# Four instead of two FFN pairs of layer 0 done plainly, seven by Strassen's algorithm, and the plain half-B blocks placed beside and behind a recurrence

## The chip, the cores and the metric

The kernel runs on one core of one Trainium2 chip. The metric is the device time of one execution in microseconds, the median of several runs. Before the change the median of three runs is 2479.92 us (2478.91 to 2481.79).

## What is computed

Two layers on a sequence of 1024 tokens of width 1024, all in float32. Layer 0 has a mixer (one input projection, gated spatial mixing, trailing means, one output projection), layer 1 is RWKV-7 time mixing, a recurrence over the tokens. After each mixer comes a SwiGLU FFN with 2816 hidden columns, and a last RMS norm ends the program.

```python
def swiglu(hn, w_gate, w_up, w_down):
    return (jax.nn.silu(hn @ w_gate) * (hn @ w_up)) @ w_down

# per layer
h = h + mixer(rms_norm(h, mix_norm[layer]))          # layer 0: gated mixing and pooling; layer 1: RWKV-7
h = h + swiglu(rms_norm(h, ffn_norm[layer]), ffn_w_gate[layer], ffn_w_up[layer], ffn_w_down[layer])
```

The recurrence of RWKV-7 in the reference is one step per token on a 64x64 state per head, 16 heads:

```python
sa = einsum('bhvk,bhk->bhv', state, a_t)
state = state * w_t + sa[..., None] * b_t + v_t[..., None] * k_t
y_t = einsum('bhvk,bhk->bhv', state, r_t)
```

## The kernel before, in words

**Products.** Each float32 operand is split into a high part (rounded to the fp32r format by ScalarE, `ACTIVATE`, L157) and the low rest (subtracted by VectorE, L158). One product is then three matmuls, high by high, low by high and high by low, `mm3` at L393 to L395 and `quarter` at L724 to L726. A weight block of 1024x128 is one 512 KB load into a tile `raw`, of which there are three, and is split into `whi` and `wlo`, three of each. The loads are issued on ScalarE's queue (L121), in the order of a list `plan`. `take(key)` hands out the next block of the list, splits the one behind it and issues the loads of up to two more.

**Halves.** The tokens are two halves, A (0 to 511) and B (512 to 1023). The FFN has 22 hidden blocks of 128 columns, or 11 pairs. With 1024 rows of contraction, a plain block costs 8 x 3 = 24 matmuls of 128x512 for each weight matrix (gate and up) and each half.

**Strassen.** A pair of blocks, both halves and both halves of the contraction are a 2x2 block product. `full_steps` does it with 7 products of 4 x 3 = 12 matmuls instead of 8 (`quarter`), after VectorE has made sums of the weights; `combine` has made the sums of the activations (`t1` to `t4`) before. The hidden blocks are written to memory (`hid_d`, L737) and read back (`hd`, L888) by the down projection.

**Stages, in the order of time.**
1. The mixer of layer 0.
2. `first_steps` over the list `FRONT`: half A of the plain pairs (`PLAIN`), and the first of the seven products of the pairs in `FIRST`, which is written to memory (`p1_d`) and read back later. Beside it `combine` runs on VectorE and ScalarE.
3. `full_steps` over `PORDER`: the pairs by Strassen, both halves.
4. The down projection of half A (`D0A`), then the first four groups of three blocks of half B (`D0B[0]`), beside which the projections of layer 1 for half A begin; then `project`, those projections.
5. `recur(0, ...)`: the recurrence of half A in 8 chunks of 64 tokens. Its matmuls are small (64x64 and the like, helper line L1456), depend on one another, and leave through VectorE, ScalarE and GpSimd. After every second chunk `post` normalises (`ysb`), and `turn_out` transposes and writes the result to `y_d` (L1681). Beside it `ffn(0, 1, ...)` does the plain blocks of half B: gate, up and down. `drive(dense, side, ratio)` writes out the two in turn, `ratio` units of recurrence for each unit of 24 dense matmuls, and gives the recurrence the higher priority.
6. `steps_b`: the rest of half B's down projection (`D0B[1]`, from `hid_d`), then the output projection of layer 1, which needs `y_d` back: four loads into `raw`, split into `ahi` and `alo` (`take_act`, called between the last matmuls of `steps_b`).
7. The same projections and recurrence for half B beside layer 1's FFN of half A, and the rest of the FFN.

**Order.** The kernel is written against pools of tiles with a scheduler that simulates the engines and picks, for each engine, the next instruction by priority among those that could go. So the order on each queue is the scheduler's. On an engine all is done in that order; an instruction that waits holds those behind it.

The lines that the change touches stand for stages 2, 3, 5 and 6:

```python
PLAIN = (0, 1)
FIRST = (2, 3)
PORDER = (4, 5, 6, 2, 7, 8, 9, 3, 10)
...
f = 2 * len(PLAIN)
D0P = [[2 * i, 2 * i + 1] for i in PLAIN]
D0B = [[a, a + 1, a + 2] for a in range(f, f + 12, 3)], [[a, a + 1] for a in range(f + 12, 22, 2)]
```

`D0P` are the groups of plain blocks of half B, `D0B` the groups of the others. With four plain blocks, `D0B[0]` is blocks 4 to 15 and `D0B[1]` is the pairs 16/17, 18/19 and 20/21. The hidden tiles of 16/17 come from a pool that is open during the recurrence; those of 18 to 21 from a pool `fy` that is opened after it, in the memory that the recurrence leaves.

Of the kernel before, what the change touches and what calls it, by code (L numbers as in the profile page):

```python
# [34 lines left out]


PAIRS = 11
PLAIN = (0, 1)
FIRST = (2, 3)
PORDER = (4, 5, 6, 2, 7, 8, 9, 3, 10)  # L40


@with_exitstack
def tile_trunk(
# [79 lines left out]
    def whl():  # L124
        return wst.tile([P, D], F32R, tag="whi", name="whi"), wst.tile([P, D], F32R, tag="wlo", name="wlo")
# [153 lines left out]
    while D0A[-1][-1] < 21:  # L279
        f = D0A[-1][-1] + 1  # L280
# [53 lines left out]
    def push_f(l, h, groups):  # L334
        return [lambda e=e: push_ffn_event(l, h, *e, lean=True) for e in ffn_events(groups)]

    push_beside(0, [lambda g=g: push_d(0, 1, [g]) for g in D0B[0]])
    push_proj(0, ("n0", n_d[0]))
    for e in push_f(0, 1, D0P):
        e()  # L340
    push_d(0, 1, D0B[1])
    o_first = push_o(0)
# [209 lines left out]
    hn = []  # L552
# [324 lines left out]
    def down_steps(h, groups, wslot, hslot, ahead=True, after=None, between=iter(()), at={}, first={}):  # L877

        held = {}
        for g in groups:  # L880
            for f in g:
                dests[h, f] = lambda f=f: wslot(f)

        def load(g):
            for f in g:
                if f not in held:
                    held[f] = hslot(f)
                    sp.dma_start(held[f].bitcast(F32), hid_d[h][:, f])  # L888

        def prime(n=1):  # L890
            for g in groups[:n]:
                load(g)

        def steps():
            for gi, g in enumerate(groups):
                load(g)
                wd = {f: take(("d", 0, h, f)) for f in g}
                if gi in at:
                    at[gi]()
                if ahead and gi + 1 < len(groups):  # L900
                    load(groups[gi + 1])
                for m in range(KT):
                    o = mmt()
                    ms = slice(m * P, (m + 1) * P)
                    for i, f in enumerate(g):
                        mm3(o, wd[f][0][:, ms], wd[f][1][:, ms], held[f][:, 0, :], held[f][:, 1, :], i == 0, i == len(g) - 1)
                    if gi == 0 and m in first:
                        dve.tensor_tensor(out=H[h][:, m, :], in0=first[m], in1=o, op=ALU.add)
                    else:
                        residual(m, h, o)  # L910
                    if after is not None and gi == len(groups) - 1:
                        after(m)
                    if gi == len(groups) - 1 and m % 2:
                        next(between, None)
                    yield len(g) / 8

        return prime, steps()
# [9 lines left out]
    def ffn(l, h, hn, fp, groups=GROUPS, last=False, nd=3, after=None, between=iter(())):  # L927
        dests["d"] = lambda: (fp.tile([P, D], F32R, tag="wdhi", bufs=nd, name="wdhi"),
                              fp.tile([P, D], F32R, tag="wdlo", bufs=nd, name="wdlo"))
        sg, hid, turned = {}, {}, []  # L930
        for kind, f in ffn_events(groups):
            if last and f in groups[-1] and len(turned) < 4 and (kind, f) != ("g", groups[-1][0]):
                turned.append(turn(h, len(turned)))
                if f == groups[-1][-1]:
                    turned += [turn(h, j) for j in range(len(turned), 4)] if kind == "u" else []
            if kind == "g":
                wg = take(("g", l, h, f))
                o = mmt()
                yield from dense_steps(o, *wg, *hn)
                sg[f] = fp.tile([P, HT], F32, tag="sg", bufs=2, name="sg")  # L940
                act.activation(sg[f], o, AF.Silu)
                next(between, None)
                yield FINE / KT
            elif kind == "u":
                wu = take(("u", l, h, f))
                o = mmt()
                yield from dense_steps(o, *wu, *hn)
                s = sg.pop(f)
                dve.tensor_tensor(out=s, in0=s, in1=o, op=ALU.mult)  # L949
                hi = fp.tile([P, HT], F32R, tag="hidhi", bufs=nd, name="hidhi")  # L950
                lo = fp.tile([P, HT], F32R, tag="hidlo", bufs=nd, name="hidlo")
                act.activation(hi, s, AF.Copy)  # L952
                dve.tensor_tensor(out=lo, in0=s, in1=hi.bitcast(F32), op=ALU.subtract)
                hid[f] = (hi, lo)
                next(between, None)
                yield FINE / KT
            else:
                wd = {}
                for ff in f:
                    wd[ff] = take(("d", l, h, ff))  # L960
                if last and f == groups[-1]:
                    yield from final_down(h, f, wd, hid, turned)
                    continue
                for m in range(KT):
                    o = mmt()
                    ms = slice(m * P, (m + 1) * P)
                    for i, ff in enumerate(f):
                        mm3(o, wd[ff][0][:, ms], wd[ff][1][:, ms], *hid[ff], i == 0, i == len(f) - 1)
                    residual(m, h, o)
                    if after is not None and f == groups[-1]:  # L970
                        after(m)
                    yield len(f) / 8
# [38 lines left out]
    def drive(dense_gen, side_gen=None, ratio=1.0):  # L1011

        due, left = 0.0, side_gen is not None

        def step():
            with tc.high_priority(offset=AHEAD):
                return next(side_gen, None)

        for weight in dense_gen:
            due += ratio * weight  # L1020
            while left and due > 0.0:
                cost = step()
                if cost is None:
                    left = False
                else:
                    due -= cost
        while left:
            left = step() is not None
# [880 lines left out]
    wp, wp_es = open_pool(name="wp0", bufs=1, side="left")  # L1909
    f, f_es = open_pool(name="ffn1", bufs=1, side="right")  # L1910
    _, hslot = slots_of(f, 0, 2)
    late = []
    spill_h = lambda m: sp.dma_start(h_d[1, 1][:, m, :], H[1][:, m, :])
    between = []
    prime_b, steps_b = down_steps(1, D0B[1], lambda f: whl(), lambda f: (hslot if f < 18 else late[0])(f), True, spill_h, (next(between[0]) for _ in range(4)))
    prime_b()
    drive(ffn(0, 1, nxt["hn"], f, D0P, nd=2), with_reload(hb_pool, 1, h_d[1, 0], recur(0, wp)), 9.3)
    wp_es.close()
    y, y_es = open_pool(name="y0", bufs=1, side="left")
    ys = open_act(("y", 0), y)  # L1920
    fy, fy_es = open_pool(name="ffn1y", bufs=1, side="left")
    late.append(slots_of(fy, 0, 4)[1])
    between.append(with_first(0))
    drive(steps_b)
    fy_es.close()
    f_es.close()
    ps_es.close()
    np_, np_es = open_pool(name="np1", bufs=1, side="right")
# [91 lines left out]
```

## Time and profile before

| what | value |
|---|---|
| median of 3 runs | 2479.92 us |
| the profiled execution: its time | 2477.8 us |
| its span, first to last instruction | 2476.1 us |
| mean granted TensorE clock | 0.981 |
| PE busy | 2371.4 us, 96% |
| DVE busy | 1496.4 us, 60% |
| ACT busy | 937.6 us, 38% |
| POOL busy | 215.5 us, 9% |
| read and written in HBM | 264.11 MB and 79.76 MB |

PE is TensorE's matmuls, PEld its weight loads, DVE is VectorE, ACT is ScalarE, POOL is GpSimd, SP is the engine that only issues DMAs. A busy time of PE is the time in which at least one matmul was under way; one 128x512 matmul is listed with about 394 ns, but the next starts some 0.227 us after it, so that the duration is not the price. "Idle before" and its releaser tell how long an engine stood still ahead of an instruction and what ended that. PEclk is the share of TensorE's full clock that was granted in that stretch.

### The profile page before, as it was taken

The page shows a single profiled execution, that of the slowest core. Times are in us where ns is not written, and L with a number is a line of the kernel's source. Part 1 is how long each engine was busy: PE and PEld are TensorE (multiplying, and loading weights), DVE is VectorE, ACT ScalarE, POOL GpSimd, SP SyncE. Part 2 cuts the span into 40 slices and gives each one's busy share as a digit, 9 for nine tenths or more (in the row PEclk, how much of TensorE's full clock was granted, in tenths as well). Part 3 has the DMA queues.
Part 4 walks back from the last instruction along what each step waited for, and adds up shares of the span by engine and source line. Part 5 has one row for each costly group of instructions (what it writes and reads, how often), then busy time and mean ns, then how long its engine had stood idle before and what let it go on. Part 6 is the DMA issues. An engine that isn't in the chain of part 4 may idle for free. (4 is left out here: it accounts for less than half of the span.)

```text
span 2476.1 us, 38179 instructions
## 1 busy us (share of the span) xinstructions
PE 2371.4 (96%) x15519; PEld 1948.0 (79%) x15519; DVE 1496.4 (60%) x2372; ACT 937.6 (38%) x1415; POOL 215.5 (9%) x246
## 2 busy tenths in 40 slices
PE   8999999999999999989869999999999999999998
PEld 7888888888787778768757778778888778888887
DVE  6446775666567947856758947855664446444444
ACT  6233453343313744423325744432331224322223
POOL 0200000000000023301100123201110000000001
PEclk9999999999999999999979999999999999999999
DMA  5124443333765455774435465693534322434231
GB/s 179 48 67 141 152 134 119 128 103 127 263 234 200 153 164 143 205 210 135 135 101 178 142 169 142 187 242 114 162 102 136 111 85 75 146 103 119 85 99 55
DMA packets 419248, 346.37 MB, mean 140 GB/s; under 512 B 94657, under 2 KB 364097, under 8 KB 418305
## 3 DMA queue, kind: packets, MB, share of 16 engines
q10 hardware_dynamic: 264000, 193.75, 25.9%
q1 hardware_dynamic: 155072, 150.18, 19.7%
q8 instruction: 122, 2.00, 0.3%
q14 instruction: 54, 0.43, 0.1%
HBM read 264.11 MB, written 79.76 MB: 139 GB/s over the span
## 5 line engine op out<-in xcount | busy, mean ns | idle before, releaser
L393 PE MATMUL mm<-ahi,whi 128*128 128x512 f32 x1312 | 516.4, 395 | 4.4 <-DVE h L487 2.4
L394 PE MATMUL mm<-alo,whi 128*128 128x512 f32 x1312 | 516.5, 394 | 1.1 <-DVE alo L158 1.1
L395 PE MATMUL mm<-ahi,wlo 128*128 128x512 f32 x1312 | 514.9, 393 | 0.5 <-DVE wlo L158 0.5
L157 ACT ACTIVATE whi<-raw 128x1024 fp32r<-128x1024 f32 (+1 forms) x276 | 274.3, 1000 | 566.1 <-PE mm L394 424.0
L158 DVE TENSOR_TENSOR wlo<-raw,whi 128x1024 fp32r<-128x1024 f32 (+1 forms) x276 | 319.2, 1160 | 195.0 <-ACT whi L157 173.2
L393 PEld LDWEIGHTS mm<-ahi,whi 128*128 128x128 f32 x1312 | 247.5, 189 | 59.5 <-ACT whi L157 4.2
L394 PEld LDWEIGHTS mm<-alo,whi 128*128 128x128 f32 x1312 | 247.3, 189 | 55.4 <-issue 2.4
L395 PEld LDWEIGHTS mm<-ahi,wlo 128*128 128x128 f32 x1312 | 247.4, 189 | 53.7 <-issue 1.4
L487 DVE TENSOR_TENSOR h<-h,mm 128x512 f32<-128x512 f32 x276 | 184.7, 684 | 169.1 <-PE mm L395 160.5
L393 PE MATMUL mm<-hidhi,wdhi 128*128 128x512 f32 x304 | 117.0, 394 | 7.1 <-ACT hidhi L952 2.9
L394 PE MATMUL mm<-hidlo,wdhi 128*128 128x512 f32 x304 | 119.0, 391 | 0.1
L395 PE MATMUL mm<-hidhi,wdlo 128*128 128x512 f32 x304 | 118.9, 391 | 0.0
L724 PE MATMUL mm<-ahi,whi 128*128 128x512 f32 x280 | 109.4, 391 | 0.0
L725 PE MATMUL mm<-alo,whi 128*128 128x512 f32 x280 | 109.0, 389 | 0.0
L726 PE MATMUL mm<-ahi,wlo 128*128 128x512 f32 x280 | 108.2, 389 | 0.0
L158 DVE TENSOR_TENSOR wdlo<-raw,wdhi 128x1024 fp32r<-128x1024 f32 x42 | 51.4, 1224 | 72.4 <-ACT wdhi L157 72.3
L157 ACT ACTIVATE wdhi<-raw 128x1024 fp32r<-128x1024 f32 x42 | 44.3, 1058 | 130.7 <-DMA raw<-in_ffn_w_down_dram 97.4
L949 DVE TENSOR_TENSOR sg<-sg,mm 128x512 f32<-128x512 f32 x48 | 32.9, 686 | 94.4 <-PE mm L395 94.3
L393 PE MATMUL mm<-hd,dhi 128*128 128x512 f32 x192 | 75.0, 392 | 4.1 <-ACT ahi L157 1.7
L394 PE MATMUL mm<-hd,dhi 128*128 128x512 f32 x192 | 75.2, 391 | 0.0
L395 PE MATMUL mm<-hd,dlo 128*128 128x512 f32 x192 | 74.1, 389 | 0.0
L393 PEld LDWEIGHTS mm<-hidhi,wdhi 128*128 128x128 f32 x304 | 57.0, 188 | 21.4 <-DVE h L487 4.4
(397 smaller groups left out, 4460.6 us busy)
## 6 DMA issues: line engine op xcount, KB each, us to landing
raw<-in_ffn_w_down_dram ACTq DMA_DIRECT2D x88, 512.0 KB
raw<-in_ffn_w_gate_dram ACTq DMA_DIRECT2D x72, 512.0 KB
raw<-in_ffn_w_up_dram ACTq DMA_DIRECT2D x72, 512.0 KB
hid_d<-hid SPq DMA_DIRECT2D x40, 512.0 KB
hd<-hid_d SPq DMA_DIRECT2D x30, 512.0 KB
raw<-in_ab_w_in_dram ACTq DMA_DIRECT2D x16, 512.0 KB
raw<-in_ab_w_out_dram ACTq DMA_DIRECT2D x16, 512.0 KB
raw<-in_rwkv_w_r_dram ACTq DMA_DIRECT2D x16, 512.0 KB
```

The source lines that it names most:

```text
L157: act.activation(hi, src, AF.Copy)
L158: (eng or dve).tensor_tensor(out=lo, in0=src, in1=hi.bitcast(F32), op=ALU.subtract)
L393: pe.matmul(o, whi, xhi, start=first, stop=False)
L394: pe.matmul(o, whi, xlo, start=False, stop=False)
L395: pe.matmul(o, wlo, xhi, start=False, stop=last)
L487: dve.tensor_tensor(out=H[h][:, m, :], in0=H[h][:, m, :], in1=o, op=ALU.add)
L724: pe.matmul(o, wh[:, k, :], x[0][:, k, :], start=st, stop=False, skip_group_check=True)
L725: pe.matmul(o, wh[:, k, :], x[1][:, k, :], start=False, stop=False, skip_group_check=True)
L726: pe.matmul(o, wl[:, k, :], x[0][:, k, :], start=False, stop=k == 3, skip_group_check=True)
L949: dve.tensor_tensor(out=s, in0=s, in1=o, op=ALU.mult)
```

## The change

Pairs 2 and 3 are plain too: blocks 0 to 7 are done plainly and pairs 4 to 10 by Strassen; no first products are written out and read back. In stage 5, three of the four groups of half B's plain blocks are beside the recurrence, with a ratio of 6.2 instead of 9.3, and the fourth is written behind it. `D0B[0]` becomes blocks 8 to 19 and `D0B[1]` the one pair 20/21, whose hidden tiles come from the pool that is open during the recurrence.

```diff
-PLAIN = (0, 1)
-FIRST = (2, 3)
-PORDER = (4, 5, 6, 2, 7, 8, 9, 3, 10)
+PLAIN = (0, 1, 2, 3)
+FIRST = ()
+PORDER = (4, 5, 6, 7, 8, 9, 10)
...
-    for e in push_f(0, 1, D0P):
+    for e in push_f(0, 1, D0P[:3]) + push_f(0, 1, D0P[3:]):
         e()
     push_d(0, 1, D0B[1])
...
-    late = []
     spill_h = lambda m: sp.dma_start(h_d[1, 1][:, m, :], H[1][:, m, :])
     between = []
-    prime_b, steps_b = down_steps(1, D0B[1], lambda f: whl(), lambda f: (hslot if f < 18 else late[0])(f), True, spill_h, (next(between[0]) for _ in range(4)))
+    prime_b, steps_b = down_steps(1, D0B[1], lambda f: whl(), hslot, True, spill_h, (next(between[0]) for _ in range(4)))
     prime_b()
-    drive(ffn(0, 1, nxt["hn"], f, D0P, nd=2), with_reload(hb_pool, 1, h_d[1, 0], recur(0, wp)), 9.3)
+    drive(ffn(0, 1, nxt["hn"], f, D0P[:3], nd=2), with_reload(hb_pool, 1, h_d[1, 0], recur(0, wp)), 6.2)
     wp_es.close()
     y, y_es = open_pool(name="y0", bufs=1, side="left")
     ys = open_act(("y", 0), y)
-    fy, fy_es = open_pool(name="ffn1y", bufs=1, side="left")
-    late.append(slots_of(fy, 0, 4)[1])
     between.append(with_first(0))
+    drive(ffn(0, 1, nxt["hn"], f, D0P[3:], nd=2))
     drive(steps_b)
-    fy_es.close()
     f_es.close()
```

How the scheduler orders it, at two places. First TensorE at the end of the recurrence of half A. Before, the last chunk's products of the state (`S`, `Q`, `uv`; `yp` is the output) and the last transposes (`ysb`) follow each other, and the next dense matmuls are those of the down projection from `hd`:

```order
L1456 MATMUL sm<-S,ar 64x64 x16
L1456 MATMUL sm<-Q,XT 64x64 x16
L1456 MATMUL yp<-S,ar 64x64 x16
L1456 MATMUL sm<-uv,bkt 64x64 x16
L1456 MATMUL yp<-uv,gt 64x64 x16
L1456 MATMUL sm<-ident,ysb 128x128 x8
L393 MATMUL mm<-hd,whi 128x512
L394 MATMUL mm<-hd,whi 128x512
L395 MATMUL mm<-hd,wlo 128x512
```

Now, the piece around the last transposes (buffer numbers kept, since the rows would read alike). Ahead of these rows stand 58 dense matmuls since the last `yp<-uv,gt`:

```order
L395 MATMUL mm_10961<-ahi_7768,wlo_10925 128x512
L393 MATMUL mm_11003<-hidhi_10918,whi_10957 128x512
L394 MATMUL mm_11003<-hidlo_10919,whi_10957 128x512
L395 MATMUL mm_11003<-hidhi_10918,wlo_10958 128x512
L393 MATMUL mm_11011<-hidhi_10918,whi_10957 128x512
L394 MATMUL mm_11011<-hidlo_10919,whi_10957 128x512
L395 MATMUL mm_11011<-hidhi_10918,wlo_10958 128x512
L1456 MATMUL sm_10820<-ident_63,ysb_10737 128x128
L393 MATMUL mm_11019<-hidhi_10918,whi_10957 128x512
```

What moved: 65 dense matmuls of the fourth plain group stand between the end of the last chunk and its first transpose, 6 more among the transposes, and after the last transpose 36 more of that group and the 48 of pair 20/21 come before the output projection. In the chunks between two `yp<-S,ar` there are now 30, 49, 36, 38, 53, 28 and 50 dense matmuls, where there were 28, 46, 41, 30, 23, 0 and 0.

Second, ScalarE where `y_d` is read back. Before (`raw_11022` and `raw_11096` hold the down weights of block 21 and the first weights of the output projection):

```order
L121 DMA raw_11105<-y_d0_82 128x1024
L157 ACTIVATE ahi_10931<-raw_11105 128x1024
L121 DMA raw_11129<-y_d0_82 128x1024
L157 ACTIVATE ahi_10931<-raw_11129 128x1024
L121 DMA raw_11133<-y_d0_82 128x1024
L157 ACTIVATE whi_11101<-raw_11022 128x1024
L157 ACTIVATE whi_11107<-raw_11096 128x1024
```

Now (`raw_10997` holds the down weights of block 21, `raw_11067` the first of the output projection):

```order
L121 DMA raw_11076<-y_d0_82 128x1024
L157 ACTIVATE ahi_10851<-raw_11076 128x1024
L157 ACTIVATE whi_11072<-raw_10997 128x1024
L157 ACTIVATE whi_11078<-raw_11067 128x1024
L121 DMA raw_11100<-y_d0_82 128x1024
L121 DMA raw_11104<-y_d0_82 128x1024
L157 ACTIVATE ahi_10851<-raw_11100 128x1024
L121 DMA raw_11126<-y_d0_82 128x1024
```

What moved: the split of block 21's down weights stands behind one load of `y_d` where it stood behind three, but there is only one group of the down projection left to cover that load, and that group needs these weights. Between the end of Strassen's products and the first matmul of the recurrence, TensorE's rows are the same in both.

## The prediction

> **What bounds the kernel now.** I read the page first: its span, and how much of it TensorE works.
>
> ```profile
> span 2476.1 us, 38179 instructions
> PE 2371.4 (96%) x15519; PEld 1948.0 (79%) x15519; DVE 1496.4 (60%) x2372; ACT 937.6 (38%) x1415; POOL 215.5 (9%) x246
> ```
>
> TensorE sets the time nearly everywhere, so a change counts by the matmuls that it adds and by the gaps between matmuls that it opens or closes. Then I took stretches of my own choice: Strassen's products (from 258.6), the recurrence of half A in three parts, its end, the down projection behind it, and for comparison the recurrence of half B.
>
> ```profile
> core 0: us, PE busy (x) PEld busy (x) DVE busy (x) ACT busy (x) POOL busy (x), PEclk, DMA share, GB/s
> 258.60:647.50 388.90, 388.41 (x1715) 320.92 (x1715) 255.91 (x383) 164.47 (x263) 1.12 (x2) 1.00 0.40 134
> 300.00:600.00 300.00, 300.00 (x1325) 248.43 (x1324) 196.12 (x296) 126.00 (x206) 0.00 (x0) 1.00 0.39 127
> 1119.40:1199.10 79.70, 78.79 (x1469) 65.47 (x1466) 55.06 (x125) 23.69 (x45) 10.17 (x11) 1.00 0.49 144
> 1199.10:1254.20 55.10, 44.96 (x1002) 40.83 (x998) 38.60 (x86) 17.14 (x38) 9.07 (x8) 0.84 0.44 124
> 1254.20:1279.50 25.30, 6.61 (x109) 5.71 (x106) 11.44 (x40) 4.44 (x11) 2.90 (x1) 0.63 0.18 54
> 1279.50:1307.30 27.80, 25.02 (x96) 19.50 (x97) 16.40 (x21) 7.74 (x9) 0.00 (x0) 0.91 0.58 200
> 1674.90:1831.80 156.90, 154.44 (x2621) 129.26 (x2618) 99.08 (x215) 48.89 (x93) 18.12 (x18) 0.99 0.43 127
> ```
>
> The third row has nothing but 128x512 matmuls: 300 us for 1324 of them, 0.2266 us each. That is my price of a dense matmul. Strassen's stretch runs at that pace throughout. The recurrence of half A does not: it is nearly full up to 1199, then falls to 82% at a clock of 0.84, and at its end to a quarter at 0.63.
>
> To see what a chunk costs I counted the dense matmuls in three stretches (one of the three in each triple, L394) and the recurrence's own (L1456). Each stretch begins and ends where a chunk's `yp<-S,ar` begins.
>
> ```profile
> 1119.40:1199.10 79.70, 19.28 (x48) 9.03 (x48) 1.00 0.49 144
> 1199.10:1254.20 55.10, 3.26 (x8) 1.50 (x8) 0.84 0.44 124
> 1674.90:1831.80 156.90, 43.50 (x108) 20.57 (x108) 0.99 0.43 127
> ...
> 1119.40:1199.10 79.70, 44.31 (x1324) 39.51 (x1321) 1.00 0.49 144
> 1199.10:1254.20 55.10, 39.83 (x979) 36.80 (x975) 0.84 0.44 124
> 1674.90:1831.80 156.90, 77.34 (x2297) 69.36 (x2294) 0.99 0.43 127
> ```
>
> With some 328 small matmuls a chunk these are 4, 3 and 7 chunks. Taking 144, 24 and 324 dense matmuls at 0.2266 off, a chunk's share of the time is (79.7-32.6)/4 = 11.8 us, (55.1-5.4)/3 = 16.6 us, and (156.9-73.4)/7 = 11.9 us. So a chunk with dense work to fill its waits costs 11.8, and one without costs 16.6, at a lower clock. The dense work of stage 5 ends three chunks too early.
>
> The end of that recurrence, in order of time:
>
> ```profile
> 1257.53 1.10 PE L1456 MATMUL yp<-uv,gt 128*64 128x64 f32 x32
> 1268.63 0.45 PE L1456 MATMUL sm<-ident,ysb 128*128 128x128 f32 x1 [10.00 <-DVE ysb L1662]
> 1270.79 1.73 PE L1456 MATMUL sm<-ident,ysb 128*128 128x128 f32 x7 [1.71 <-DVE ysb L1662]
> 1271.70 2.16 DVE L1678 SCALAR_TENSOR_TENSOR gch<-sm,vec,gch 128x128 f32<-128x128 f32 x8 [1.06 <-PE sm L1456]
> 1273.88 0.53 SPq L1681 DMA_DIRECT2D y_d<-gch  x1
> ...
> 1278.12 0.34 ACTq L121 DMA_DIRECT2D raw<-y_d  x1
> 1279.56 0.80 PE L393 MATMUL mm<-hd,whi 128*128 128x512 f32 x1 [7.05 <-DMA hd<-hid_d]
> 1280.16 0.63 PE L394 MATMUL mm<-hd,whi 128*128 128x512 f32 x1
> ...
> 1284.42 0.41 PE L395 MATMUL mm<-hd,wlo 128*128 128x512 f32 x1
> ...
> 1285.09 1.06 ACT L157 ACTIVATE ahi<-raw 128x1024 fp32r<-128x1024 f32 x1 [15.90 <-DMA raw<-y_d]
> ...
> 1287.44 0.33 ACTq L121 DMA_DIRECT2D raw<-y_d  x1
> ...
> 1291.01 1.06 ACT L157 ACTIVATE ahi<-raw 128x1024 fp32r<-128x1024 f32 x1 [4.86 <-DMA raw<-y_d]
> ...
> 1301.34 1.06 ACT L157 ACTIVATE ahi<-raw 128x1024 fp32r<-128x1024 f32 x1 [3.50 <-DMA raw<-y_d]
> ```
>
> TensorE stands for 10.0 us until the normalised output is there, for 1.7 in its transposes, and for 7.05 until `hd` of blocks 18 to 21 arrives: that load goes into memory that the recurrence had held, so it is issued only at its end. The next dozen matmuls then start 0.43 apart.
>
> **The change, part by part.** *More matmuls.* A weight matrix of a pair takes 7 x 12 matmuls by Strassen and 8 x 12 plainly. Two pairs and two matrices make 48 more: 48 x 0.2266 = +10.9 us. They come as 144 fewer in stages 2 and 3 (-32.6 us, in a stretch without gaps) and 192 more around the recurrence (+43.5).
>
> *The chunks.* In the order, all seven stretches between two chunks now have 28 to 53 dense matmuls. The seven cost 4 x 11.8 + 3 x 16.6 = 97.0 us before, and at 11.85 each 83.0: -14.0 us. The ends: 11.1, in which the recurrence's own matmuls alone were busy (44.31/4), gives -19; 16.6 for all gives +19. I take the middle of the two filled rows, since the same instructions ran there.
>
> *The end.* From 1254.2 to 1307.3 are 53.1 us. Their work is 96 dense matmuls, 21.8 us, and the rest of the last chunk, which costs little when the clock is full:
>
> ```profile
> 1204.19 1.15 PE L1456 MATMUL sm<-uv,bkt 128*64 128x64 f32 x32
> 1206.20 1.09 PE L1456 MATMUL sm<-ident,bk 128*128 128x128 f32 x8
> 1221.01 1.04 PE L1456 MATMUL yp<-S,ar 64*64 64x64 f32 x30
> ```
>
> With two groups of 32 at the pace of that `yp` (1.1 each), one of `uv,bkt` and eight transposes that is 4.4 us. So 53.1-21.8-4.4 = 26.9 us are lost. Now 65 dense matmuls (14.7 us) stand ahead of the first transpose, which covers the 10.0 us; `hd` of pair 20/21 is loaded before the recurrence; so no load waits for the recurrence's memory any more. I take -26.9, and what comes back of it in the next part.
>
> *What is late next.* The loads of `y_d` stand on ScalarE's queue, and behind the first of them the split of block 21's down weights, which the matmuls need. From the last transpose, at 1272.5 in the rows above: `y_d` is issued 1.4 later, its first load 5.6 later, that load lands after 3.6 (1287.44 to 1291.01), its split takes 1.1 and the weights' 1.0 (half of the first row below): 11.3 us. VectorE has a weight split ahead of `gch` (second row, 1.2):
>
> ```profile
> 1294.76 2.01 ACT L157 ACTIVATE whi<-raw 128x1024 fp32r<-128x1024 f32 x2 [2.69 <-PE mm L394]
> ...
> L158 DVE TENSOR_TENSOR wlo<-raw,whi 128x1024 fp32r<-128x1024 f32 (+1 forms) x276 | 319.2, 1160 | 195.0 <-ACT whi L157 173.2
> ```
>
> That makes 12.5. TensorE has 36 + 6 dense matmuls until then, 9.5 us. So a new wait of +3.0 us. Its ends: nothing, if the dense work runs late itself; or 6.4, if the first load takes the 7.0 it took at 1278.12, and 2.4 more for 12 matmuls at 0.43. I take 3.0, since the four `hd` loads that shared that moment are gone.
>
> [...] The row: after 7.05 us of waiting the matmuls ran at half pace until 1284.4. [...]
>
> *At nothing.* Spills and reloads of first products and of four hidden blocks go; their cover is a TensorE that is full there (388.41 of 388.90). `combine` lies beside 384 dense matmuls instead of 288, and the stretch where it fills VectorE (next rows, first) already costs TensorE nothing; were that cover gone, 24.88 of 25 us of VectorE would show. The down projection has nine groups in half B as before. The wait at the start of the recurrence (second row) stays, as the orders of TensorE and SP there are the same.
>
> ```profile
> 275.00:300.00 25.00, 25.00 (x112) 20.68 (x111) 24.88 (x38) 12.73 (x19) 0.00 (x0) 1.00 0.57 189
> ...
> 1104.14 1.06 PE L1456 MATMUL sm<-XT,gt 32*32 32x32 f32 x32 [7.29 <-ACT bkt L1514]
> ```
>
> *Sum:* +10.9 -14.0 -26.9 +3.0 = -27.0 us. The profiled execution took 2477.8 us (span 2476.1), the median is 2479.92, 2.1 above it; taken off the median: 2453.
>
> **Rivals.** *Slower: a filled chunk costs as much as an empty one.* More dense work puts more splits and residual adds on VectorE and ScalarE, and a chunk's steps queue behind them. If all seven cost 16.6, the sum is 10.9 + 7 x 16.6 - 97.0 - 26.9 + 3.0 = +6.2: 2486. It decides from 15.7 us a chunk. For it: VectorE is busy 69% in the filled stretch, and one chunk of half B, with 42 dense matmuls (the second row counts L394), came to 17.2:
>
> ```profile
> 1713.80:1740.50 26.70, 24.34 (x385) 19.66 (x381) 13.83 (x24) 7.73 (x11) 2.54 (x3) 0.94 0.60 180
> ...
> 1713.80:1740.50 26.70, 5.96 (x14) 2.92 (x14) 0.94 0.60 180
> ```
>
> Against it: the mean of the filled ones is 11.8 and 11.9 in two stretches, with that one in. 0.04.
>
> *Faster, but the output projection waits for `y_d`.* Before, the last piece was split 25.5 us after the first load's issue (1278.12 to 1301.34, and 2.3 for its two halves). Issued at 6.8 after the last transpose, that is 32.3. TensorE by then has 84 dense matmuls, the wait of 3.0 and 18 matmuls of the output projection that need only earlier pieces: 26.1. So 6.2 us more, and 2.4 at half pace: -18.4, or 2462. For it: 96 matmuls covered these loads before, now 48 and 36. Against it: two of the loads now stand next to each other in the order. [...] 0.22.
>
> *The start's wait goes too.* If the reload of `h` comes earlier relative to the first adds, 7.3 us and some half-pace matmuls go: 2444. The orders speak against it. 0.05.
>
> *No change to speak of.* Stages 2 and 3 do not shorten by 32.6 us because VectorE's sums of weights become the bound: it would need 24 us of new gaps in a stretch where VectorE is busy 256 of 389 us. 0.04; the time then is about 2478.
>
> **How the numbers follow.** The forecast, 2453, has 0.65; its own range is 2447 to 2459, from the wait at nothing and the chunks 0.4 us cheaper, to the wait at 6.4 with half pace. What this kernel's measurement can tell from no change is about 0.2%, 5 us. Forecast, `y_d` and start are faster: 0.92; no change 0.04; slower 0.04. The range takes in the start's wait on one side and `y_d` with 2 us beyond it on the other: 2443 to 2464.
>
> **What would show it.** Strassen's stretch should last some 33 us less at 0.227 a matmul. The recurrence of half A should take about 16 us longer from its first to its last small matmul, with PE near full in every 25 us and a clock of 1.00 past its start. The waits on `ysb` (11.7 us in two before) and the 7.05 on `hd` should be gone, and one of about 3 us on `whi` or `wlo` ahead of the down projection of 20/21 should be new. I am wrong if a filled chunk's share is over 13 us, if waits of over 5 us stand between the last transpose and the output projection, or if Strassen's stretch has gaps.

## The result and the profile after

The changed kernel takes 2465.49 us (median of 4 runs, 2461.21 to 2468.91) where the kernel before took 2479.41 on the same chip: a ratio of 0.9941, 95% interval 0.9926 to 0.9956, or 13.9 us less. The forecast was 27 us less, 2453, in a range of 2443 to 2464. The sign was right, the time lies 1.5 us outside the range, and half of the forecast gain is missing. The profiled execution is the fastest of the four (2461.21 us). In two runs further on, one of the kernel before and one of the regrouped kernel, the execution took nearly twice as long (4742.88 and 4764.77 us); all medians leave these out.

The page of the changed kernel, its span and its TensorE line:

```profile
span 2459.5 us, 38177 instructions
PE 2369.8 (96%) x15567; PEld 1942.6 (79%) x15567; DVE 1474.8 (60%) x2328; ACT 934.0 (38%) x1403; POOL 216.8 (9%) x246
```

There are 48 more matmuls in 1.6 us less busy time; the mean granted clock is 0.990 where it was 0.981. The stretches of it that answer to those of the prediction: Strassen's products, the seven chunk intervals of half A's recurrence, its end in two parts (up to the last small matmul, then to the first matmul of the output projection), and the third chunk interval of half B's recurrence.

```profile
core 0: us, PE busy (x) PEld busy (x) DVE busy (x) ACT busy (x) POOL busy (x), PEclk, DMA share, GB/s
258.60:615.40 356.80, 356.11 (x1574) 294.27 (x1573) 221.01 (x323) 148.66 (x235) 1.13 (x2) 1.00 0.39 128
1086.80:1235.40 148.60, 143.75 (x2580) 120.56 (x2577) 100.04 (x218) 47.36 (x90) 18.11 (x18) 1.00 0.49 141
1235.40:1261.00 25.60, 25.37 (x201) 20.39 (x196) 16.48 (x42) 10.59 (x19) 2.90 (x1) 1.00 0.19 63
1261.00:1284.20 23.20, 20.25 (x85) 15.31 (x86) 17.11 (x28) 7.69 (x9) 0.00 (x0) 1.00 0.52 169
1693.70:1725.30 31.60, 24.00 (x387) 19.97 (x385) 14.52 (x25) 9.32 (x13) 2.51 (x3) 0.84 0.55 165
```

And the dense matmuls L394 alone (one of three) in the seven intervals and in the third of half B:

```profile
1086.80:1235.40 148.60, 37.88 (x95) 17.85 (x95) 1.00 0.49 141
1693.70:1725.30 31.60, 7.02 (x15) 3.39 (x15) 0.84 0.55 165
```

The first four rows are as wanted. Strassen's stretch is 32 us shorter and still full; the seven chunks run at a clock of 1.00; behind them TensorE is busy 25.37 of 25.60 us, where before it stood for 10 us. The last row is what the prediction did not look for: in a stage whose code is unchanged, a chunk takes 31.60 us at a clock of 0.84; in the kernel before it took 26.70 at 0.94, with 43 dense matmuls in the order of either.

From the timelines come the places of a few events, in us from the start of the span. The second trace of the changed kernel is that of the first experiment.

| event | before | after | after, second trace |
|---|---|---|---|
| end of Strassen's products | 647.4 | 615.1 | 615.6 |
| first small matmul of half A's recurrence | 1088.8 | 1057.0 | 1058.3 |
| first matmul of the output projection | 1307.4 | 1284.2 | 1288.4 |
| first small matmul of half B's recurrence | 1641.1 | 1619.2 | 1625.1 |
| end of the span | 2476.1 | 2459.5 | 2468.2 |

Up to the output projection the changed kernel is 23.2 and 19.0 us ahead. From there to half B's recurrence it loses 1.3 and 3.0, and from the start of that recurrence to the end (835.0 us before) 5.3 and 8.1.

What VectorE did in that third chunk, before and then after, by the timeline:

```profile
1718.38 1.22 DVE L158 TENSOR_TENSOR wdlo<-raw,wdhi 128x1024 fp32r<-128x1024 f32 x1 [2.27 <-ACT wdhi L157]
1719.64 1.29 DVE L1503 TENSOR_TENSOR gt<-sm,gm 128x512 f32<-128x512 f32 x2
1720.85 0.68 DVE L1595 TENSOR_TENSOR Q<-S,sm 128x512 f32<-128x512 f32 x1
1724.99 1.22 DVE L158 TENSOR_TENSOR wdlo<-raw,wdhi 128x1024 fp32r<-128x1024 f32 x1 [3.47 <-ACT wdhi L157]
```

```profile
1697.26 1.23 DVE L158 TENSOR_TENSOR wdlo<-raw,wdhi 128x1024 fp32r<-128x1024 f32 x1 [1.87 <-ACT wdhi L157]
1698.52 1.29 DVE L1503 TENSOR_TENSOR gt<-sm,gm 128x512 f32<-128x512 f32 x2
1704.84 1.23 DVE L158 TENSOR_TENSOR wdlo<-raw,wdhi 128x1024 fp32r<-128x1024 f32 x1 [5.03 <-ACT wdhi L157]
1705.98 0.68 DVE L1595 TENSOR_TENSOR Q<-S,sm 128x512 f32<-128x512 f32 x1
```

The same instructions, two of them exchanged. `Q` of L1595 is the first half of the state's update (L1596 is the second). Before, it went right behind `gt`. After, a down weight's split (`wdlo`) stands ahead of it; that waits 5.03 us for ScalarE's half of the split, which waits for a load, as ScalarE's row shows. TensorE then stands for 6.20 us, and the next dense matmuls start 0.43 us apart:

```profile
1703.75 1.06 ACT L157 ACTIVATE wdhi<-raw 128x1024 fp32r<-128x1024 f32 x1 [6.52 <-DMA raw<-in_ffn_w_down_dram]
...
1706.71 1.12 PE L1456 MATMUL sm<-ident,ysb 128*128 128x128 f32 x4 [6.20 <-DVE Q L1595]
...
1708.48 0.63 PE L393 MATMUL mm<-ahi,whi 128*128 128x512 f32 x1
1708.91 0.63 PE L394 MATMUL mm<-alo,whi 128*128 128x512 f32 x1
```

`Q` started at 1705.98, as the split that stood ahead of it came to its end (1704.84 and 1.23), and VectorE did nothing else in the 5.03 us for which that split waited.

So the theory is: the change does nearly what was forecast where it was made, and the scheduler, which orders the whole program anew, put one late split ahead of the state's update in half B's recurrence. Its rival: the loss is no matter of this order, and the change is simply worth 14 us.

### The profile page after: what moved, and what is told of

Its sections match the earlier page's. It is cut to its first block, busy times and chain, and to the rows that moved or that the text cites. A ratio compares the mean times of both kernels' runs of the same rounds, so it can differ in the third digit from the quotient of the medians.

```text
span 2459.5 us, 38177 instructions
## 1 busy us (share of the span) xinstructions
PE 2369.8 (96%) x15567; PEld 1942.6 (79%) x15567; DVE 1474.8 (60%) x2328; ACT 934.0 (38%) x1403; POOL 216.8 (9%) x246
## 4 chain that ended last, share of the span: by engine, by line
PE 77%; DVE 9%; DMA 7%; ACT 3%; issue 2%; POOL 1%; ACTq 1%; SPq 0%; POOLq 0%; DVEq 0%
PE mm L393 16%; PE mm L394 16%; PE mm L395 16%; PE mm L724 5%; PE mm L726 5%; PE mm L725 5%; PE sm L1456 5%; DVE wlo L158 1%; DMA raw<-in_ffn_w_down_dram 1%; DMA raw<-y_d 1%; PE yp L1456 1%; DVE h L487 1%; DVE mix L1163 1%; ACT whi L157 1%; PE aux L1377 1%
## 5 line engine op out<-in xcount | busy, mean ns | idle before, releaser
L393 PE MATMUL mm<-ahi,whi 128*128 128x512 f32 x1376 | 541.5, 394 | 5.3 <-DVE h L487 2.8
L394 PE MATMUL mm<-alo,whi 128*128 128x512 f32 x1376 | 542.2, 394 | 1.1 <-DVE alo L158 1.1
L395 PE MATMUL mm<-ahi,wlo 128*128 128x512 f32 x1376 | 540.6, 393 | 1.1 <-DVE wlo L158 1.1
L157 ACT ACTIVATE whi<-raw 128x1024 fp32r<-128x1024 f32 (+1 forms) x280 | 281.8, 1013 | 597.1 <-PE mm L394 448.6
L158 DVE TENSOR_TENSOR wlo<-raw,whi 128x1024 fp32r<-128x1024 f32 (+1 forms) x280 | 328.9, 1179 | 216.2 <-ACT whi L157 201.1
L393 PEld LDWEIGHTS mm<-ahi,whi 128*128 128x128 f32 x1376 | 259.2, 188 | 62.9 <-ACT whi L157 5.7
L395 PEld LDWEIGHTS mm<-ahi,wlo 128*128 128x128 f32 x1376 | 259.4, 189 | 57.7 <-issue 2.2
L394 PEld LDWEIGHTS mm<-alo,whi 128*128 128x128 f32 x1376 | 259.4, 189 | 57.5 <-issue 2.4
L487 DVE TENSOR_TENSOR h<-h,mm 128x512 f32<-128x512 f32 x276 | 185.1, 684 | 164.9 <-PE mm L395 156.7
L394 PE MATMUL mm<-hidlo,wdhi 128*128 128x512 f32 x304 | 119.0, 392 | 0.1
L724 PE MATMUL mm<-ahi,whi 128*128 128x512 f32 x296 | 115.6, 390 | 0.0
L725 PE MATMUL mm<-alo,whi 128*128 128x512 f32 x296 | 115.2, 389 | 0.0
L726 PE MATMUL mm<-ahi,wlo 128*128 128x512 f32 x296 | 113.6, 389 | 0.0
L394 PE MATMUL mm<-hd,dhi 128*128 128x512 f32 x192 | 75.1, 391 | 0.0
```

The lines of the kernel that those rows point to most:

```text
L157: act.activation(hi, src, AF.Copy)
L158: (eng or dve).tensor_tensor(out=lo, in0=src, in1=hi.bitcast(F32), op=ALU.subtract)
L393: pe.matmul(o, whi, xhi, start=first, stop=False)
L394: pe.matmul(o, whi, xlo, start=False, stop=False)
L395: pe.matmul(o, wlo, xhi, start=False, stop=last)
L487: dve.tensor_tensor(out=H[h][:, m, :], in0=H[h][:, m, :], in1=o, op=ALU.add)
```

## The experiments

Times are medians; each ratio is to the kernel before on the same chip (2481 to 2483 us there). The kernels ran in three sets on two chips, so 1 or 2 us between kernels of different sets tell nothing. Where a kernel's edit adds lines, its line numbers are up to three or four higher than those of the kernel before.

**The changed kernel again.**

> The changed kernel unedited, for a second trace and more times. Theory 1: about 8 us of the forecast's 27 are lost in half B's recurrence, whose code is unchanged, because the split of a down weight now stands ahead of the third chunk's state add on VectorE. It expects about 222 us from first to last of that recurrence's small matmuls (216 before), one chunk near 31.5 us (26.8 before), and a wait of TensorE of about 6 us ahead of that chunk's transposes. Theory 2: the loss is spread over run-to-run differences of transfers and falls elsewhere in another execution; then this recurrence is back near 216 us in some execution and the time is still about 2465. Median 2465 by both.

2467.25 us (2466.40 to 2470.11), 0.9942 [0.993, 0.9954]. Theory 1 holds in the second trace: 33.6 us for the third chunk, and 7.92 us of waiting ahead of its transposes, again for `Q` behind a split. That recurrence lasted 223.7 us (222.1 in the first trace, 215.8 in the kernel before). The wait differs between the two executions, and the chunk with it.

**Another grouping, with and without the change.** In layer 1's groups beside half B's recurrence:

```diff
-[rest[i : i + 3] for i in range(0, len(rest), 3)]
+[rest[:1]] + [rest[i : i + 3] for i in range(1, len(rest), 3)]
```

> The changed kernel, with layer 1's blocks beside half B's recurrence grouped as one and then threes instead of threes from the start. In the order the state add of the third chunk then stands ahead of the weight split on VectorE, as in the kernel before. Theory 1 (the order costs 6 to 8 us): half B's recurrence 216 us or less, median 2457 to 2460. Theory 2 (the loss is elsewhere): no gain over the changed kernel beyond 2 us, 2463 to 2467.

> The kernel before with the same regrouping, so that half B's recurrence stands in the same order as in a_first. Theory 1: about the same as before, 2477 to 2482, so that a_first is 20 to 23 us faster than b_first. Theory 2: a_first is 13 to 16 us faster than b_first, as the changed kernel is than the kernel before.

2499.83 us with the change (2497.50 to 2512.34) and 2527.93 without. Both expectations for the times failed: the grouping itself costs 33 us with the change and 46 without, at the end of half B's recurrence. The difference of the two, 28.1 us, is above what either theory expects, and it settles nothing, since that end ran differently in the two traces (windows from the last `yp<-S,ar` but one to the last, with the change and without):

```profile
1791.90:1860.00 68.10, 65.50 (x425) 41.94 (x423) 19.51 (x29) 12.93 (x18) 0.00 (x0) 0.72 0.25 71
```

```profile
1820.30:1872.80 52.50, 50.42 (x427) 34.60 (x423) 19.31 (x29) 12.93 (x18) 0.00 (x0) 1.00 0.31 92
```

The clock was 0.72 in one and 1.00 in the other; more on that in the last section. What the pair does show is the third chunk itself: with the change and this grouping, `Q` stood right behind `gt` in it, and it took 23.7 us at a clock of 1.00 instead of 31.60 at 0.84.

**One subtraction moved to GpSimd, with and without the change.** The low part of one down weight (layer 1, half A, block 3); in the order no weight split stands right ahead of the third chunk's `Q` any more:

```diff
-        splits.get(key[0], lambda i, *t: split(*t))(key[1], view(raw), view(hi), view(lo))
+        if key[0] == "d" and key[1:3] == (1, 0) and key[3] in (3,):
+            split(view(raw), view(hi), view(lo), pool)
+        else:
+            splits.get(key[0], lambda i, *t: split(*t))(key[1], view(raw), view(hi), view(lo))
```

> The changed kernel with the low part of one down weight (layer 1, half A, block 3) subtracted by GpSimd instead of VectorE; in the order no weight split then stands right ahead of the third chunk's state add. Theory 1: the 31.5 us chunk is 26 us or less, the recurrence 214 to 218 us, median 2457 to 2460. Theory 2: within 2 us of the changed kernel. A third way: GpSimd's subtraction is so slow that the matmuls of block 3 wait for it, and the time is over 2467.

> The kernel before with the same GpSimd subtraction as a_pool3, so that both have half B's recurrence in nearly one order. Theory 1 (the change itself gives 20 us or more up to that recurrence, and a reordering there gave 8 back): a_pool3 is 20 to 26 us faster than this one, and this one is at most 4 us faster than before, 2476 to 2482. Theory 2 (the GpSimd subtraction helps any version by 9 us, and the change gives only 14): this one is near 2473, and a_pool3 14 to 16 us faster than it.

With the change 2457.96 us (2455.46 to 2460.15), 0.9899 [0.9885, 0.9913]; without it 2482.35, 0.9996 [0.9985, 1.0007]. The same edit gains 9.3 us in the changed kernel and nothing in the kernel before, and between the two the change is worth 24.4 us. Theory 1 holds and its rival, by which the change is worth 14 us in any order, falls. The third chunk with the change, by windows, then VectorE's rows in it:

```profile
1694.40:1716.30 21.90, 21.90 (x386) 18.53 (x384) 14.86 (x23) 8.45 (x13) 2.51 (x3) 1.00 0.71 213
```

```profile
1696.42 1.29 DVE L1506 TENSOR_TENSOR gt<-sm,gm 128x512 f32<-128x512 f32 x2 [0.51 <-PE sm L1459]
1697.63 0.68 DVE L1598 TENSOR_TENSOR Q<-S,sm 128x512 f32<-128x512 f32 x1
```

21.90 us, all of it busy, at full clock. From the start of that recurrence to the end of the span are 834.4 us, as before (835.0). The subtraction on GpSimd lay elsewhere (at 1628.4, 2.4 us long); what helped is that the splits around the third chunk were ordered anew. The limit of this proof is that the edit moved more rows of that stage than the two; the second chunk, too, went from 22.5 to 19.4 us. In the kernel before it shortened the third chunk as well, from 26.7 to 23.7 us, and that came back within the same stage: from the recurrence's start to the end it was 837.7 us there, against 835.0.

**The kernel before with all its hidden blocks read back early.** Blocks 16 to 21 into the pool that is open during half A's recurrence:

```diff
-    _, hslot = slots_of(f, 0, 2)
+    _, hslot = slots_of(f, 0, 6)
...
-    ... lambda f: (hslot if f < 18 else late[0])(f), True, ...
+    ... hslot, True, ...
-    fy, fy_es = open_pool(name="ffn1y", bufs=1, side="left")
-    late.append(slots_of(fy, 0, 4)[1])
...
-    fy_es.close()
```

> The kernel before (two plain pairs, nothing else changed) with the hidden blocks 16 to 21 read back into the pool that is open during half A's recurrence. In the order the down projection of half B (264 dense matmuls) then moves into that recurrence, 41, 37, 37, 23, 48, 33 and 45 in its seven chunks, and none are left behind its last transposes. No matmul is added. From the prediction's own rows: the chunks cost 83 instead of 97 us; behind the last chunk the waits of 10.0 and 1.7 us stay, and the output projection waits for the output's way through memory, 13 to 25 us, in place of the 7.05. In the third chunk of half B's recurrence the weight split now stands ahead of the state add, as in the changed kernel: theory 1 expects that chunk at 30 us or more and 5 to 8 us lost there, together 2472 to 2482; if that order costs nothing, the chunk is 27 us and the time 2465 to 2474.

2485.05 us, 1.0015 [1.0003, 1.0026]: slower by a little, 3 us above the expected range. It is the reverse test, since here the bad order came into a kernel without the change. The third chunk (windows), its wait, and VectorE's rows ahead of the end of that wait:

```profile
1712.10:1744.50 32.40, 24.19 (x387) 20.04 (x383) 14.46 (x25) 9.33 (x13) 2.51 (x3) 0.84 0.55 161
```

```profile
PE sm L1456 <- DVE Q L1595: 6.1, 1, 6.1
```

```profile
1724.06 1.23 DVE L158 TENSOR_TENSOR wdlo<-raw,wdhi 128x1024 fp32r<-128x1024 f32 x1 [4.92 <-ACT wdhi L157]
1725.20 0.68 DVE L1595 TENSOR_TENSOR Q<-S,sm 128x512 f32<-128x512 f32 x1
```

32.40 us at 0.84, as in the changed kernel. From the start of that recurrence to the end of the span it is 845.8 us, 10.8 more than in the kernel before; that is more than the 5 to 8 expected, and puts the time above the range. The first half did what the filling of chunks promised: the output projection starts at 1295.4 instead of 1307.4. The wait on `ysb` stayed, as expected; the wait for the output's way through memory, expected at 13 to 25 us, was 4.3 ahead of the output projection. From the end of the last transpose to the output projection 9.9 us went by, with the few matmuls of the next norm in between (TensorE's waits from 1268 to 1313):

```profile
PE sm L1456 <- DVE ysb L1662: 11.6, 2, 9.9
PE mm L393 <- ACT ahi L157: 4.8, 2, 4.3
...
```

In the output projection itself smaller waits on `ahi`, `alo` and the weights follow. From its start to half B's recurrence 7.3 of the 12.0 us are lost again; those waits are a part of that, the rest was not taken apart. So up to half B's recurrence the filling of the chunks was worth 4.7 us in this kernel, where nothing is left to cover what comes behind the last chunk.

**Three plain pairs instead of four**, from the changed kernel with the moved subtraction:

```diff
-PLAIN = (0, 1, 2, 3)
-FIRST = ()
-PORDER = (4, 5, 6, 7, 8, 9, 10)
+PLAIN = (0, 1, 2)
+FIRST = (3,)
+PORDER = (4, 5, 6, 3, 7, 8, 9, 10)
```

> a_pool3 with three plain pairs instead of four, the fourth by Strassen with a first product spilled (24 matmuls of 0.2266 fewer, 5.4 us). All seven chunks of half A's recurrence still have 24 to 45 dense matmuls in the order, but only 6 are left between its last transpose and the output projection, where 84 were. Theory 1 (what counts besides the filled chunks is work that covers the way of the output through memory): a new wait of 10 to 20 us ahead of the output projection, time 2463 to 2473. Theory 2 (only the filling of the chunks counts): 2452 to 2454.

2466.74 us (2463.20 to 2468.61), 0.9934 [0.9921, 0.9946], 8.8 us more than with four pairs although 24 matmuls fewer are done. The time is in theory 1's range. TensorE's waits from 1262 to 1312:

```profile
PE mm L396 <- ACT ahi L160: 4.1, 1, 4.1
PE aux L431 <- DVE nacc L410: 4.1, 1, 4.1
PE mm L396 <- DMA hd<-hid_d: 3.2, 1, 3.2
PE mm L396 <- ACT whi L160: 2.4, 2, 1.2
PE mm L397 <- DVE alo L161: 2.3, 2, 1.9
```

Together 16.1 us, but not one wait, and not all for the output's way: `hd` is a load of hidden blocks, `nacc` the sums of the next norm, drawn in while the output was not there, and `whi` the split of weights. Ahead of the output projection the output itself costs the 4.1 on `ahi`, and the 4.1 on `nacc` beside it. The whole stretch says the same: from the first small matmul of half A's recurrence to the output projection it is 214.0 us instead of 228.1, 14.1 less, where the 96 dense matmuls that are gone from it are worth 21.8. The seven chunks cost 12.0 us each besides their dense work in both, so the fourth pair pays by what it covers behind them, not by filling chunks.

**All four groups written beside the recurrence**, from the same kernel:

```diff
...
-    drive(ffn(0, 1, nxt["hn"], f, D0P[:3], nd=2), with_reload(hb_pool, 1, h_d[1, 0], recur(0, wp)), 6.2)
+    drive(ffn(0, 1, nxt["hn"], f, D0P[:4], nd=2), with_reload(hb_pool, 1, h_d[1, 0], recur(0, wp)), 4.65)
...
-    drive(ffn(0, 1, nxt["hn"], f, D0P[3:], nd=2))
```

> a_pool3 with all four groups of half B's plain blocks written beside the recurrence at a ratio of 4.65 and none behind it. In the order the dense matmuls of the seven chunks are 30, 49, 36, 38, 53, 40, 52 instead of 30, 49, 36, 38, 53, 28, 50: the scheduler draws the work in by priority wherever it is written. So 2456 to 2460 if the amount of dense work counts; if what is written behind counts (cover of the last transposes and of the output's way through memory), 10 us or more slower.

2457.98 us, 0.9903 [0.9887, 0.9918], the same within the intervals. Where the fourth group is written made no difference here; by the order only 14 of its matmuls moved into the chunks, since the scheduler draws them in by priority either way.

**The reload of `h` three steps later**, from the same kernel. `k` starts at -6 instead of 0, and a load is issued only where it is not negative.

```diff
-        k = 0
+        k = -6
         for cost in side:
-            if k < KT:
+            if 0 <= k < KT:
                 sp.dma_start(H[h][:, k : k + 2, :], src[:, k : k + 2, :])
-                k += 2
+            k += 2
```

> a_pool3 with the reload of h issued three steps of the recurrence later. At the start of the recurrence TensorE waits 7 us for ScalarE's copies bkt; in the order these stand behind a weight load on ScalarE's queue that waits for the semaphore of an earlier transfer of h. Here that semaphore belongs to a small transfer. If that is the cause, the 7 us wait is gone and the time is 2450 to 2455, unless the adds into h wait instead (then 2458). If the copies wait for something else, 2456 to 2460.

2451.87 us (2450.61 to 2455.89), 0.9879 [0.9865, 0.9892]: the fastest of all, 31.3 us less than the kernel before in the same set. At the start of the recurrence ScalarE's queue, in the changed kernel (with the moved subtraction the same releaser is named, after 8.45 us) and then here (a DMA issue, then the copies behind it):

```profile
1071.38 0.37 ACTq L121 DMA_DIRECT2D raw<-in_ffn_w_gate_dram  x1
1071.81 1.08 ACT L1514 ACTIVATE bkt<-sm 128x512 f32<-128x512 f32 x2 [8.73 <-DMA h<-h_d]
```

```profile
1069.52 0.38 ACTq L121 DMA_DIRECT2D raw<-in_ffn_w_gate_dram  x1
1069.94 1.08 ACT L1517 ACTIVATE bkt<-sm 128x512 f32<-128x512 f32 x2 [5.86 <-DMA XT<-xi_d]
```

The copies that TensorE waits for do not need `h`. They stand behind the issue of a weight load, and that issue waits for another transfer, `h` in one case and the small `XT` in the other, as the releasers say. TensorE's wait is 4.2 us instead of 6.9, and 1.4 for the adds into `h` is new. So the cause is as expected, and the wait is shorter, not gone. The gain is 6.1 us by the medians and 5.0 by the ratios, and the two waits explain 1.3 of it; the rest (a recurrence with another share of dense matmuls) was not taken apart.

**The output's low parts on GpSimd**, on top of the kernel with the moved subtraction, and on top of the later reload:

```diff
+    splits[("y", 0)] = lambda _, *t: split(*t, pool)
```

> a_pool3 with the low parts of the four pieces of half A's output subtracted by GpSimd. The 48 matmuls of the down projection behind half A's recurrence start 0.287 us apart, and TensorE waits there for VectorE's adds into h, which stand behind these subtractions. If that is the cause, the 48 go at 0.23 to 0.25 and the time is 2 to 3 us less, 2455 to 2456. If GpSimd's 2.4 us instead of 1.2 makes the last piece late, the output projection waits 1 to 4 us more: 2458 to 2462.

> p_hd3 with the same four subtractions on GpSimd. By the first reading 2449 to 2451, by the second 2452 to 2456.

2461.84 us, 0.9913 [0.9897, 0.993], and 2455.47, 0.9895 [0.988, 0.9911]: no gain in either. Both times lie in the ranges of the second reading, but not for its reason. The 48 matmuls went at 0.282 instead of 0.294 us in the first and at 0.240 instead of 0.267 in the second, which is 0.6 and 1.3 us. The output projection was not late for it: from the start of the recurrence to it are 228.3 us instead of 228.1 and 220.4 instead of 221.0. But from the start of half B's recurrence to the end both are longer, by 3.3 and 10.6 us, and in the fourth chunk of it TensorE waited for VectorE's `gt` (the rows of the first, then of the second):

```profile
PE sm L1460 <- DVE gt L1507: 4.1, 1, 4.1
```

```profile
PE sm L1460 <- DVE gt L1507: 3.8, 1, 3.8
```

It stood behind splits of down weights there. Whether GpSimd's work had a part in that was not tried.

## Why the prediction was right in half and wrong in half

The sum had -27.0 us. Against the profiled execution before, the two traces of the changed kernel give these:

| step of the sum | forecast | first trace | second trace |
|---|---|---|---|
| fewer matmuls in stages 2 and 3 | -32.6 | -32.3 | -31.8 |
| from there to half A's recurrence | 0 | +0.5 | +1.3 |
| recurrence to output projection (+43.5 - 14.0 - 26.9 + 3.0) | +5.6 | +8.6 | +11.5 |
| from there to half B's recurrence | 0 | +1.3 | +3.0 |
| half B's recurrence and the rest | 0 | +5.3 | +8.1 |
| sum | -27.0 | -16.6 | -7.9 |

The second trace is of an execution of 2469.92 us, 2.7 above its median, and the trace before of one below its own, so the medians lie between: -13.9 in the first set of runs, -15.1 in the second.

*More matmuls.* Right. Strassen's stretch is 356.80 us, 1560 of its matmuls are products, 144 fewer than before, and none of the covers costed at nothing there failed. The wait at the start of the recurrence stayed too, as said, at 7.21 us (7.29 before).

*The chunks.* Right. The seven intervals are 148.60 us with 95 times three dense matmuls: (148.6 - 285 x 0.2266)/7 = 12.0 us a chunk, where 11.85 was forecast and 16.6 was the price of empty ones: 1 us too low in all. In the second trace the fifth chunk alone costs 1.6 more. The rival by which a filled chunk is as dear as an empty one is out.

*The end, and what is late next.* The waits on `ysb` (11.7) and `hd` (7.05) are gone. Of the 48.8 us from the last `yp<-S,ar` to the output projection, 172 dense matmuls by the order (39.0) and the 4.4 of the last chunk leave 5.4 lost, where 3.0 was forecast. The waits there are these:

```profile
PE mm L393 <- DVE h L487: 2.6, 3, 1.0
PE mm L393 <- ACT whi L157: 0.3, 1, 0.3
```

The wait on `whi` that the step worked out is 0.3, not 3.0, and `y_d` was never waited for, so that rival is out too. The sum left the clock alone behind its wait of 3.0 us; no run shows that such a wait does so, and of eleven waits of 2.1 to 2.9 us in two traces six were followed by half pace (last section). Here no wait was over 1.0 us. In place of the forecast wait the last 48 matmuls, which make an output for VectorE's add into `h` (L487) every six, start 0.287 us apart instead of 0.227; that is 2.9 of the 5.4 us, and the other 2.5 were not taken apart. I put this down to the splits of `alo` and `wlo` among those adds, and the runs bear that out in part at most: with `alo` on GpSimd the pace went to 0.282 in one kernel and to 0.240 in the other. That 2.9 comes near the forecast 3.0 is luck, since its cause was another.

*The step that failed* is one that the sum did not have: half B's recurrence and the stage ahead of it have unchanged code and were put at nothing, without a reason given. The list of what was costed at nothing named the covers of the removed and moved work, not the order in the stages behind it. That order was there to be read, and on VectorE two instructions of one chunk were exchanged in it. From half B's recurrence to the end 5.3 and 8.1 us were lost in the two traces, and the third chunk alone is 4.9 and 6.9 longer than before (31.6 and 33.6 against 26.7). The pair with the moved subtraction shows it: without this exchange, and with what else that edit moved, the change is worth 24.4 us, against 27.0 forecast. In the first trace the miss of 10.4 us is these 5.3, 3.0 from the two sizes above (1.0 and 2.4 too low, less 0.4 elsewhere), and 2.1 from the other rows of the table. The 1.3 to 3.0 us lost between the output projection and half B's recurrence lie among single waits of TensorE of 1 to 3 us, on VectorE and ScalarE and in the first trace also on a load (`bk`, 1.8), and were not taken apart.

The range was wrong with it. It had both ends from terms at the place of the change, and nothing for a stage that the scheduler might order anew; the two traces price that at 5 to 8 us.

## What to carry to other kernels

When a scheduler orders a program, an edit in one stage can order the others anew: compare the order of every stage where an engine is waited for, not of the edited ones alone, and look for an instruction that waits for a load and has come ahead of a step that others wait for. Where work is added to fill gaps, count also what covers the chain behind the last gap; with two and three plain pairs the chunks were filled as well, and much of the gain was lost again behind them. A wait behind a DMA issue on a busy engine's queue can belong to a transfer that the waiting engine does not need (here 8.73 us of ScalarE, for `h`).

## What the runs showed of the hardware

Equal waits were followed by matmuls at different paces. The same wait of 2.64 us ahead of the same matmul, in the kernel with the moved subtraction and then in the second trace of the changed kernel:

```profile
1318.11 0.77 PE L396 MATMUL mm<-ahi,whi 128*128 128x512 f32 x1 [2.64 <-DVE h L490]
1318.67 0.63 PE L397 MATMUL mm<-alo,whi 128*128 128x512 f32 x1
1319.10 0.63 PE L398 MATMUL mm<-ahi,wlo 128*128 128x512 f32 x1
```

```profile
1321.11 0.47 PE L393 MATMUL mm<-ahi,whi 128*128 128x512 f32 x1 [2.64 <-DVE h L487]
1321.42 0.39 PE L394 MATMUL mm<-alo,whi 128*128 128x512 f32 x1
```

In one the next six start 0.43 us apart, in the other at once 0.23. In the first traces of the kernel before and of the changed kernel, leaving out the first wait of each program, all nine waits of 3.9 us or more were followed by matmuls at half pace. After eight of them the clock was back 4.0 to 6.6 us behind the end of the wait; the longest, of 10.00 us, was followed by half pace up to the next wait. Of the eleven waits of 2.1 to 2.9 us in these two traces six were followed by half pace, one of them only 2.3 us later, and five were not, the longest (2.92, ahead of 1981.85 in the kernel before) among them.

In one execution the clock also dropped with no wait close ahead of it. In the regrouped kernel with the change, pairs of small matmuls (32x32, and 64x64 from 1820.8) stand between single dense ones from 1815.6 to 1851.8, and the clock falls to half at 1818.6, with no wait of TensorE in the 18 us ahead of that (from 1796 to 1826 PEclk is 0.88, and the one wait is of 1.8 us for `gt`). In the window from 1826 to 1860, which takes in 8 us of other work at its end, TensorE is busy throughout, and PEclk is 0.56; some rows of the sequence follow:

```profile
1826.00:1860.00 34.00, 34.00 (x131) 19.55 (x132) 5.06 (x6) 3.72 (x5) 0.00 (x0) 0.56 0.06 18
```

```profile
1825.67 0.79 PE L393 MATMUL mm<-ahi,whi 128*128 128x512 f32 x1
1826.39 0.47 PE L1456 MATMUL sm<-uv,gt 64*64 64x64 f32 x2
1826.80 0.79 PE L394 MATMUL mm<-alo,whi 128*128 128x512 f32 x1
```

A dense matmul with its pair takes 1.13 us there. Without the change the same sequence ran at a clock of 1.00, at 0.69 (1848.01 to 1848.70):

```profile
1848.01 0.51 PE L395 MATMUL mm<-ahi,wlo 128*128 128x512 f32 x1
1848.45 0.33 PE L1456 MATMUL sm<-uv,gt 64*64 64x64 f32 x2
1848.70 0.50 PE L393 MATMUL mm<-ahi,whi 128*128 128x512 f32 x1
```

Even that is over twice the 0.2266 us of a dense matmul and the 0.07 of two small ones in a row of 32 (1.1 us). Why was not tried; that a dense matmul with its pair took 0.69 and 1.13 us there, and that the clock was at half with TensorE busy, are what these rows show.
